# One-hot tiles a token at a time, gates stored expert by expert: the expert stage of a two-block network on one Trainium2 core

## The chip, the cores and the metric

The kernel runs on one core of a Trainium2 chip. The metric is the device time of one launch in microseconds, and lower is better. The core has a TensorE for matrix products, VectorE and ScalarE (ACT) and GpSimd (POOL) for the rest, and DMA queues that SyncE, ACT and POOL issue to. The times given are medians of several launches.

## What is computed

The reference is a pipeline of two blocks on 512 tokens of 1024 features, all in float32. The first has two layers of retention and attention with a feed-forward part. The second has a gated delta rule beside a recurrent unit, a cross attention into a memory, and a layer of retrieved experts, to which the change belongs:

```python
def peer_ffn(h, wq, subkeys, u_tab, v_tab):
    q = (t @ wq).reshape(ntok, 8, 2, 128)                    # 8 heads, two halves of a query
    sc = einsum('thpd,hpkd->thpk', q, subkeys)               # against 128 first and 128 second keys
    s1, i1 = top_k(sc[:, :, 0], 16); s2, i2 = top_k(sc[:, :, 1], 16)
    best, pos = top_k(s1[..., :, None] + s2[..., None, :], 16)     # of 256 pairs
    idx = e1 * 128 + e2                                      # e1, e2: i1, i2 at pos // 16, pos % 16
    gate = softmax(best)
    act = gelu(einsum('phkd,pd->phk', u_tab[idx], t)) * gate
    return einsum('phk,phkd->pd', act, v_tab[idx])
```

There are 16384 experts (128 first keys times 128 second keys), and a token uses 8 x 16 of them.

## The kernel before

**The expert stage.** The tokens stand in four blocks of 128. The last block gathers its experts' rows by indirect DMA. The first three (384 tokens, dense) are multiplied with both whole tables: `first_product(j)` is the product of the 128 experts of first key j with the dense tokens (24 passes 384 wide, as each float32 operand is carried as a high and a low part), and `second_product` adds up the second table's rows. Between them stands a factor for every expert and token: the token's gate where it uses the expert, zero elsewhere.

**The choices** (2384 to 2523 us). `choose` finds a head's 16 best pairs for 128 tokens on VectorE. At its end the keys of the chosen pairs are picked out of a list: a 16x16 comparison (L1692), a multiplication on POOL (L1694), and a reduction over 16 on VectorE (L1695). It runs for all eight heads of the first block and for four heads of the second and third. The others, eight in all, run during the spreading, and eight more for the gathered block later.

**The spreading** (2523 to 2765 us). `spread(n)` makes the table of factors of a dense block. A token's factors over 128 first and 128 second keys are a product of two matrices that the token's 128 choices index: `oa` has a row for each choice with its gate at the place of the second key, `ob` a one at the place of the first key. `ones_hot` makes both for four tokens at a time (32 blocks for each n, 96 in all): two comparisons on VectorE, 512 wide, of the row `io` (0 to 127) with the choice's key (L1774, L1775). The gate is then multiplied into `oa`, in every second block by four activations on ACT (L1778), in the others by one operation on POOL (L1780). Two blocks later TensorE multiplies the four tokens' `oa` and `ob` into a bank of PSUM (L1795), ACT moves it to a staging tile `st` (L1797), and after eight blocks SyncE stores that to DRAM as `gd` (L1801). Products of the first table fill TensorE in between. Their tile of weights is split by `load_w`: the high part by ACT (L243), the low part by POOL here, and by VectorE for the third block of tokens (L244).

**The second tables** (from 2765 us). `prepare(j)` loads `gin` from `gd` for four first keys at a time, multiplies the acts of tile j by it (L1873), and splits the result (L331 on ACT, L332 on VectorE). `second_product` (L1883) follows. The gathered block's rows come in beside it (L1853, L1859, L1862).

Each engine takes its instructions in the order in which they were given to it. A tile's buffers are written again only when their readers are done.

Of the kernel before, what the change touches and what calls it, by code (L numbers as in the profile page):

```python
# [29 lines left out]
# ------------------------------------------------------------------ host side: layout only  # L30
def _wtiles(w):
    """[K, M] -> [M/128, 128, (K/128)*128]; each tile holds all of K for 128 columns."""
    k, m = w.shape
    return w.reshape(k // 128, 128, m // 128, 128).transpose(2, 1, 0, 3).reshape(m // 128, 128, -1)


def _vtiles(w):
    """[1024, N] -> [(N/256)*2, 128, 4*256]; halves of K for 256 columns."""
    n = w.shape[1]
    return w.reshape(2, 4, 128, n // 256, 256).transpose(3, 0, 2, 1, 4).reshape(-1, 128, 1024)  # L40
# [24 lines left out]
def _vec(a):  # L65
    """[..., 128*n] -> [128, ..., n]"""
    a = a.reshape(a.shape[:-1] + (-1, 128))
    return np.moveaxis(a, -1, 0)
# [52 lines left out]
def _blockdiag(w):  # L121
    """[8, 64, 64] -> [128, 4, 128]: two blocks to a chunk"""
    o = np.zeros((4, 128, 128), w.dtype)
    o[:, :64, :64] = w[0::2]
    o[:, 64:, 64:] = w[1::2]
    return o.transpose(1, 0, 2)
# [29 lines left out]
# ------------------------------------------------------------------ the program  # L156
def interleave(*gens):
    """Emit the steps of several strands in turns; a pair gives a strand and its steps to a turn."""
    live = [g if isinstance(g, tuple) else (g, 1) for g in gens]
    while live:  # L160
        for g in list(live):
            if any(next(g[0], "end") == "end" for _ in range(g[1])):
                live.remove(g)
# [22 lines left out]
def _program(tc, I, out, dbg, upto, layers, pools):  # L186
# [32 lines left out]
    def rsqrt_small(dst, src, scale):  # L219
        """dst = (src*scale + EPS)^-0.5 for a narrow [p, n]."""  # L220
# [6 lines left out]
    def load_w(src=None, sub=None, pool=None, into=None):  # L227
        """a tile of weights, as the sum of two that a pass each carries"""
# [18 lines left out]
    def pieces(p, n):  # L247
        """[128, n] in a tile of PG, as pieces of up to a bank"""
        return [p[:, 0, :HN], p[:, 1, :HN]] if n == L else [p[:, 0, :n]]

    def PV(p, n):
        """the same, as one"""
# [23 lines left out]
    def fed_gemms(feed_c, u, n, fills=()):  # L276
        """Products of the next three tiles of weights with u, following its chunks as feed_c writes them, after
        other ones that wait for nothing; returns what they are in, as pieces of up to a bank."""
# [35 lines left out]
    # ---------------------------------------------------------------- first block  # L314
# [9 lines left out]
    def V2(t):  # L324
        """what matches PV"""
        return t.rearrange("p (a b) -> p a b", a=2) if t.shape[1] == L else t

    def split(dh, dl, src, g=None, on=None):
        """dh + dl = src (* g)"""
# [27 lines left out]
    def cols6(acc, scale):  # L357
        """rsqrt(mean over partitions) per token, blocks of tokens as columns"""
# [8 lines left out]
    def bcast6(r6):  # L367
        """the same as rows, all partitions alike: slices of the tokens and where they are"""
# [26 lines left out]
    def cols(acc, scale, n):  # L395
        """rsqrt(mean over partitions) per token, [128, n/128]"""
# [7 lines left out]
    def bcast(r):  # L404
        """[128, k] -> rows [128, k*128] in PSUM, the same on all partitions"""
# [20 lines left out]
    # the memory's keys and values, a tile at a time where the first block leaves the tensor engine room  # L426
# [32 lines left out]
    def memory_values(ng, mem):  # L459
        """two steps"""  # L460
# [19 lines left out]
    # the first layer's input, and its first products  # L480
# [7 lines left out]
    def products_aside(feed_c, n, scale=1.0, fills=(), room=None):  # L488
        """the first four tiles of a phase, put aside until the tokens' scales are there"""
# [27 lines left out]
    for l in range(layers):  # L517
# [3 lines left out]
        # from here on the last layer leaves the first tokens out, except as keys and values  # L521
# [5 lines left out]
        # ============================================================ phase A  # L527
# [10 lines left out]
        # distances: between tokens of a block, and down a column to the block's ends  # L538
# [11 lines left out]
        # decays of a block's keys towards its end and its start, and of a whole block (of the sums from the  # L550
        # tokens before in the upper half, from those after in the lower)
# [6 lines left out]
        # what turns the distances' decays into those to a block's ends  # L558
# [3 lines left out]
        # the tokens' scales as columns, for the blocks of TB  # L562
# [12 lines left out]
        # the attention's keys, split in two: the first parts of a group twice, the rests once  # L575
# [3 lines left out]
        # a block of queries makes room for its own outputs; the other half holds what retention cycles through  # L579
        QA = OA = QO[:, 0]  # L580
        spare = QO[:, 1].rearrange("p a b -> p (a b)")
        # keys of one head of a chunk, with zeros for the other; a head's queries with both decays
# [7 lines left out]
        def scaled(tab):  # L590
            """a table times the tokens' scales"""
# [34 lines left out]
        # values, turned to token-major; the retention's minus their mean over a head's features, so that  # L626
        # its outputs have mean zero
# [24 lines left out]
        # the first tokens' values of a group, block diagonal over its heads  # L652
# [16 lines left out]
        # ---- projections that fill in: queries and keys of the attention, then the retention's gates  # L669
# [25 lines left out]
        # ---- retention: within a block of tokens as it stands, between blocks by the decayed sums of keys  # L695
        # times values over the blocks before and after
        def retention():
# [35 lines left out]
            def turn(c):  # L733
                """a chunk's keys, token-major"""
# [67 lines left out]
        # ---- attention over the first tokens and a band  # L802
        def halves(qb):
            """a block's queries, a group's first parts and rests above each other"""
# [123 lines left out]
        # ============================================================ phase B  # L928
# [59 lines left out]
        def spaced_rs(ss, name, fills):  # L988
            """the tokens' scales, with other products between their steps"""
# [77 lines left out]
        if l == layers - 1:  # L1067
            # the delta rule's decays and steps
# [9 lines left out]
    # ---------------------------------------------------------------- second block  # L1078
# [28 lines left out]
    def softplus(dst, x, n):  # L1107
        """log(1 + exp(x)) = max(x, 0) + 2 atanh(e / (2 + e)), e = exp(-|x|)"""
# [15 lines left out]
    # decay and step of a token and head as columns, [128, 4 (block), 4 (head)]  # L1124
# [30 lines left out]
    def conv(dst, p, w, bias=None, on=None, soon=False):  # L1155
        """causal taps along the tokens of p * row scale"""
# [31 lines left out]
    def gate(c, p):  # L1188
        """the delta rule's"""
# [61 lines left out]
    # ---- the remaining projections fill in: the recurrence's input and gate, the delta rule's gate  # L1251
# [19 lines left out]
    # ---- the gated delta rule, a block of 128 tokens and four heads at a time; what a block needs of the  # L1271
    # others comes last, and replaces its queries, keys and values
    def inside(n, e):
# [31 lines left out]
        # the inverse of I + A, and its transpose, by doubling of the blocks  # L1305
# [101 lines left out]
    # ---- the gated linear recurrence  # L1407
# [47 lines left out]
    # ---- out of the mixer: the first tiles, over the recurrence's outputs, while the delta rule ends  # L1455
# [51 lines left out]
    # ---- attention into the memory  # L1507
# [84 lines left out]
    # ---- product-key experts: the first three blocks of tokens against the whole tables, the last by gathers  # L1592
    def head_queries(h):
        """of a head, both sides; without the tokens' scales"""
# [26 lines left out]
    gd = dr.tile([ND, 128, 32, 128, 4], F32, name="gd")  # L1621
# [30 lines left out]
    def sixteens(pool):  # L1652
        """0 to 15 down, the same along"""
# [5 lines left out]
    def selection(pool, bufs):  # L1659
        """the tiles of a block's choices: their sums, and the keys of both sides"""  # L1660
# [4 lines left out]
    def choose(pool, sel, h, sc):  # L1665
        """the 16 best pairs of keys of a head, of scores [128, 2, 128]"""
# [28 lines left out]
        nc.vector.tensor_reduce(keys[:, :, h], oh.rearrange("p s j k -> p s k j"), axis=AX.X, op=OP.add)  # L1695

    def soften(n, best):
        """softmax over a head's 16, of scores still without the tokens' scales, in place"""
# [8 lines left out]
    # acts of a tile of 128 experts (one first key) for the dense tokens  # L1707
# [22 lines left out]
    BYACT = lambda k: k % 2 == 0  # L1730
    sels = [selection(p1, ND) for n in range(ND)]
    fill = iter(range(LA))
    # the first block's choices come first; the second and third one's last four heads wait till it is spread
# [26 lines left out]
    # the experts' weights of a block's tokens, spread over all experts: [second key, first key, token]  # L1760
    def spread(n):
# [8 lines left out]
        def ones_hot(b, by_act):  # L1770
            oa = p1.tile([128, 4, 128], F32, name="oa", tag="oa", bufs=5)
            ob = p1.tile([128, 4, 128], F32, name="ob", tag="ob", bufs=5)
            iot = io[:, None, :].to_broadcast([128, 4, 128])
            nc.vector.tensor_tensor(oa, iot, sl[:, 2, b:b + 4, None].to_broadcast([128, 4, 128]), op=OP.is_equal)  # L1774
            nc.vector.tensor_tensor(ob, iot, sl[:, 1, b:b + 4, None].to_broadcast([128, 4, 128]), op=OP.is_equal)  # L1775
            if by_act:
                for t in range(4):
                    nc.scalar.activation(oa[:, t], oa[:, t], AF.Copy, scale=sl[:, 0, b + t:b + t + 1])  # L1778
            else:
                nc.gpsimd.tensor_tensor(oa, oa, sl[:, 0, b:b + 4, None].to_broadcast([128, 4, 128]), op=OP.mult)  # L1780
# [3 lines left out]
        for k in range(32 + LEAD):  # L1784
            if k < 32:
                hot.append(ones_hot(4 * k, BYACT(k)))
# [3 lines left out]
            if m % 8 == 0:  # L1790
                st = p1.tile([128, 32, 32, 4], F32, name="stg", tag="stage", bufs=2)
# [5 lines left out]
            nc.scalar.activation(st[:, :, t0:t0 + 4], pg4.rearrange("p (t g e) -> p g t e", t=4, e=4), AF.Copy)  # L1797
# [161 lines left out]
```

## Time and profile before

| | us |
|---|---|
| time, median of 3 runs | 3728.36 |
| lowest and highest of the 3 | 3717.03, 3739.03 |
| the profiled execution: its span, first to last instruction | 3726.1 |

The profiled execution's own launch time is not listed apart from the three; its span is 2.3 us below their median.

The page gives each engine's busy time over the span. A table of stretches gives it stage by stage, with the granted clock of TensorE and the share of the DMA engines. The waits say which engine waited for whose result. Groups of instructions say how often an operation ran and its mean time, in which waiting for a shared resource is included; start-to-start times in the timeline show what an instruction really takes of its engine, as the next one starts before the end of the one ahead is recorded.

### The profile page before, as it was taken

The page shows a single profiled execution, that of the slowest core. Times are in us where ns is not written, and L with a number is a line of the kernel's source. Part 1 is how long each engine was busy: PE and PEld are TensorE (multiplying, and loading weights), DVE is VectorE, ACT ScalarE, POOL GpSimd, SP SyncE. Part 2 cuts the span into 40 slices and gives each one's busy share as a digit, 9 for nine tenths or more (in the row PEclk, how much of TensorE's full clock was granted, in tenths as well). Part 3 has the DMA queues.
Part 4 walks back from the last instruction along what each step waited for, and adds up shares of the span by engine and source line. Part 5 has one row for each costly group of instructions (what it writes and reads, how often), then busy time and mean ns, then how long its engine had stood idle before and what let it go on. Part 6 is the DMA issues. An engine that isn't in the chain of part 4 may idle for free. (4 is left out here: it accounts for less than half of the span.)

```text
span 3726.1 us, 54318 instructions
## 1 busy us (share of the span) xinstructions
PE 3586.0 (96%) x21341; PEld 3212.1 (86%) x21341; DVE 2413.2 (65%) x4258; ACT 1494.8 (40%) x2675; POOL 946.7 (25%) x708
## 2 busy tenths in 40 slices
PE   8999999999999999999999999997889999999998
PEld 8989999999997888788878877887778999999987
DVE  7554436333656454633467755689979988888875
ACT  4454324222444432422344453425553434434333
POOL 4211112000422111200032330446433334333321
PEclk9988999999998999999999999998999999999999
DMA  4101232222320033322232131323468878888855
GB/s 138 58 23 41 93 119 97 90 89 89 124 86 29 30 105 116 101 96 96 93 123 68 35 96 55 116 86 119 130 209 323 338 304 320 315 320 324 317 212 181
DMA packets 185887, 531.42 MB, mean 143 GB/s; under 512 B 16416, under 2 KB 70048, under 8 KB 168992
## 3 DMA queue, kind: packets, MB, share of 16 engines
q1 hardware_dynamic: 150272, 367.67, 29.6%
q0 software_dynamic: 18432, 134.23, 9.1%
q10 hardware_dynamic: 16928, 26.06, 2.1%
q8 instruction: 168, 2.75, 0.3%
q14 instruction: 87, 0.71, 0.1%
HBM read 492.64 MB, written 35.19 MB: 142 GB/s over the span
## 5 line engine op out<-in xcount | busy, mean ns | idle before, releaser
L243 ACT ACTIVATE whi<-wraw 128x1024 fp32r<-128x1024 f32 x594 | 627.6, 1058 | 1043.0 <-PE g L263 628.3
L244 DVE TENSOR_TENSOR wlo<-wraw,whi 128x1024 fp32r<-128x1024 f32 x543 | 680.5, 1254 | 294.9 <-ACT whi L243 287.6
L263 PE MATMUL g<-uh,whi 128*128 128x264 f32 (+1 forms) x1864 | 476.1, 318 | 4.6 <-ACT z L605 4.6
L263 PE MATMUL g<-uh,wlo 128*128 128x264 f32 (+1 forms) x1864 | 468.7, 314 | 1.3 <-DVE wlo L244 1.3
L263 PE MATMUL g<-ul,whi 128*128 128x264 f32 (+1 forms) x1864 | 468.8, 314 | 0.0
L350 POOL TENSOR_TENSOR ssq<-ssq,sq 128x512 f32<-128x512 f32 (+2 forms) x84 | 133.4, 1588 | 926.1 <-issue 715.8
L1721 PE MATMUL f<-TH,wlo 128*128 128x384 f32 x1024 | 348.8, 341 | 5.4 <-POOL wlo L244 5.4
L1721 PE MATMUL f<-TH,whi 128*128 128x384 f32 x1024 | 350.8, 343 | 1.2 <-ACT stash L1722 1.1
L1721 PE MATMUL f<-TL,whi 128*128 128x384 f32 x1024 | 347.5, 339 | 0.0
L263 PEld LDWEIGHTS g<-uh,whi 128*128 128x128 f32 x1864 | 308.4, 192 | 25.4 <-ACT z L605 5.0
L263 PEld LDWEIGHTS g<-uh,wlo 128*128 128x128 f32 x1864 | 307.7, 191 | 21.4 <-DVE wlo L244 1.6
L263 PEld LDWEIGHTS g<-ul,whi 128*128 128x128 f32 x1864 | 308.2, 191 | 19.6 <-issue 1.3
L1904 POOL COPY pace<-al 1x1 f32<-1x1 f32 x128 | 109.4, 855 | 563.6 <-DVE al L332 561.8
L1883 PE MATMUL acc<-whi,ah 128*128 128x512 f32 x768 | 240.1, 394 | 7.3 <-ACT whi L243 6.4
L1883 PE MATMUL acc<-wlo,ah 128*128 128x512 f32 x768 | 238.9, 392 | 4.1 <-DVE wlo L244 4.1
L1883 PE MATMUL acc<-whi,al 128*128 128x512 f32 x768 | 238.5, 392 | 0.0
L263 PE MATMUL g<-Hh,wlo 128*128 128x264 f32 (+1 forms) x768 | 203.9, 320 | 0.0
L263 PE MATMUL g<-Hl,whi 128*128 128x264 f32 (+1 forms) x768 | 203.8, 320 | 0.0
L263 PE MATMUL g<-Hh,whi 128*128 128x264 f32 (+1 forms) x768 | 203.4, 319 | 0.0
L1853 POOL DMA_INDIRECT gtile<-in_uv_dram,ix x128 | 189.8, 1483 | 46.4 <-issue 27.4
L1721 PEld LDWEIGHTS f<-TH,whi 128*128 128x128 f32 x1024 | 196.2, 192 | 5.8 <-ACT stash L1722 1.9
L1721 PEld LDWEIGHTS f<-TH,wlo 128*128 128x128 f32 x1024 | 195.5, 191 | 6.4 <-POOL wlo L244 6.4
(588 smaller groups left out, 7608.3 us busy)
## 6 DMA issues: line engine op xcount, KB each, us to landing
wraw<-in_w_dram SPq DMA_DIRECT2D x340, 512.0 KB, 3.5
wraw<-in_uT_dram SPq DMA_DIRECT2D x128, 512.0 KB, 5.6
wraw<-in_uv_dram SPq DMA_DIRECT2D x128, 512.0 KB, 4.9
gd<-stg SPq DMA_DIRECT2D x12, 2048.0 KB, 9.9
gin<-gd SPq DMA_DIRECT2D x32, 768.0 KB, 11.2
h0c<-in_h_dram SPq DMA_DIRECT2D x8, 264.0 KB, 4.3
H<-in_h_dram ACTq DMA_DIRECT2D x8, 264.0 KB, 5.9
hs<-H ACTq DMA_DIRECT2D x8, 264.0 KB, 2.1
```

The source lines that it names most:

```text
L243: nc.scalar.activation(hi, raw, AF.Copy)
L244: (sub or nc.vector).tensor_tensor(lo, raw, hi.bitcast(F32), op=OP.subtract)
L263: nc.tensor.matmul(pw, wt[:, sl], xt[:, kc, hf * w_:(hf + 1) * w_], start=(first and n == 0 and a == 0), stop=(last and n == len(kcs) - 1 ...
L350: nc.gpsimd.tensor_tensor(self.acc, self.acc, t, op=OP.add)
L1721: nc.tensor.matmul(p[:, :NT], wt[:, sl], x[:, kc], start=(kc == 0 and a == 0), stop=(kc == 7 and a == 2))
L1853: nc.gpsimd.indirect_dma_start(out=gtile, out_offset=None, in_=I["uv"], in_offset=bass.IndirectOffsetOnAxis(ap=ix[:, k:k + 1], axis=0))
L1883: nc.tensor.matmul(accs[2 * n + q], x[:, tk], wt[:, 512 * q:512 * q + 512], start=(j == 0 and k == 0), stop=(j == 127 and k == 2))
L1904: after = nc.gpsimd.tensor_copy(pace, ready[2][0:1, 0:1].bitcast(F32)).ins
```

## The change

It touches four places, all in the expert stage. `ones_hot` makes the tiles for one token at a time: for each of four tokens one scalar operation 128 wide compares `io` with the key of each partition and multiplies by the gate, and one compares with the other key. The activations on ACT and the multiplications on POOL are gone. The staging tile, `gd` and `gin` put a first key's tokens next to each other, in runs of 32, where four first keys alternated token by token. The product with `gin` reads those runs. In `choose`, the reduction over 16 becomes four additions that halve the list each time. Comments and docstrings are removed as well, which lie outside the program that the chip runs.

```diff
-    gd = dr.tile([ND, 128, 32, 128, 4], F32, name="gd")
+    gd = dr.tile([ND, 128, 32, 4, 128], F32, name="gd")
...
-        nc.vector.tensor_reduce(keys[:, :, h], oh.rearrange("p s j k -> p s k j"), axis=AX.X, op=OP.add)
+        for n in (8, 4, 2):
+            nc.vector.tensor_tensor(oh[:, :, :n], oh[:, :, :n], oh[:, :, n:2 * n], op=OP.add)
+        nc.vector.tensor_tensor(keys[:, :, h], oh[:, :, 0], oh[:, :, 1], op=OP.add)
...
-    BYACT = lambda k: k % 2 == 0
...
-        def ones_hot(b, by_act):
+        def ones_hot(b):
             oa = p1.tile([128, 4, 128], F32, name="oa", tag="oa", bufs=5)
             ob = p1.tile([128, 4, 128], F32, name="ob", tag="ob", bufs=5)
-            iot = io[:, None, :].to_broadcast([128, 4, 128])
-            nc.vector.tensor_tensor(oa, iot, sl[:, 2, b:b + 4, None].to_broadcast([128, 4, 128]), op=OP.is_equal)
-            nc.vector.tensor_tensor(ob, iot, sl[:, 1, b:b + 4, None].to_broadcast([128, 4, 128]), op=OP.is_equal)
-            if by_act:
-                for t in range(4):
-                    nc.scalar.activation(oa[:, t], oa[:, t], AF.Copy, scale=sl[:, 0, b + t:b + t + 1])
-            else:
-                nc.gpsimd.tensor_tensor(oa, oa, sl[:, 0, b:b + 4, None].to_broadcast([128, 4, 128]), op=OP.mult)
+            for t in range(4):
+                k = slice(b + t, b + t + 1)
+                nc.vector.tensor_scalar(oa[:, t], io, sl[:, 2, k], sl[:, 0, k], op0=OP.is_equal, op1=OP.mult)
+                nc.vector.tensor_scalar(ob[:, t], io, sl[:, 1, k], None, op0=OP.is_equal)
             return oa, ob
...
-                hot.append(ones_hot(4 * k, BYACT(k)))
+                hot.append(ones_hot(4 * k))
...
-                st = p1.tile([128, 32, 32, 4], F32, name="stg", tag="stage", bufs=2)
+                st = p1.tile([128, 32, 4, 32], F32, name="stg", tag="stage", bufs=2)
...
-            nc.scalar.activation(st[:, :, t0:t0 + 4], pg4.rearrange("p (t g e) -> p g t e", t=4, e=4), AF.Copy)
+            nc.scalar.activation(st[:, :, :, t0:t0 + 4], pg4.rearrange("p (t g e) -> p g e t", t=4, e=4), AF.Copy)
...
-                nc.sync.dma_start(gd[n, :, :, 32 * q:32 * q + 32], st)
+                nc.sync.dma_start(gd[n, :, :, q], st.rearrange("p g e t -> p g (e t)"))
...
-            gins[0] = p2.tile([128, ND, 128, 4], F32, name="gin", tag="gin", bufs=2)
-            nc.sync.dma_start(gins[0], gd[:, :, j // 4].rearrange("n p t e -> p n t e"))
+            gins[0] = p2.tile([128, ND, 4, 4, 32], F32, name="gin", tag="gin", bufs=2)
+            nc.sync.dma_start(gins[0].rearrange("p n q e t -> p n (q e t)"),
+                              gd[:, :, j // 4].rearrange("n p q x -> p n (q x)"))
...
-        nc.vector.tensor_mul(a, a, gins[0][:, :, :, j % 4].rearrange("p n t -> p (n t)"))
+        a4 = a.rearrange("p (n q t) -> p n q t", n=ND, q=4)
+        nc.vector.tensor_mul(a4, a4, gins[0][:, :, :, j % 4])
```

## Rows read from the trace of the kernel before

**Rows 1.** The page's busy time, share of the span and instructions of each engine.

```profile
PE 3586.0 (96%) x21341; PEld 3212.1 (86%) x21341; DVE 2413.2 (65%) x4258; ACT 1494.8 (40%) x2675; POOL 946.7 (25%) x708
```

**Rows 2.** Stages: stretch, length, busy PE, PEld, DVE, ACT, POOL; clock, DMA share, GB/s.

```profile
2384.00:2523.00 139.00, 126.73 (x649) 111.71 (x648) 124.61 (x527) 44.88 (x69) 68.58 (x38) 0.97 0.29 95
2523.00:2700.00 177.00, 144.83 (x891) 139.19 (x890) 167.30 (x355) 98.42 (x228) 98.01 (x54) 0.90 0.42 125
2700.00:2765.00 65.00, 56.14 (x391) 54.57 (x389) 59.33 (x68) 45.36 (x111) 29.83 (x19) 0.95 0.60 179
2765.00:2900.00 135.00, 124.53 (x614) 112.00 (x613) 112.24 (x175) 47.39 (x77) 38.32 (x30) 0.96 0.90 317
2900.00:3713.00 813.00, 812.07 (x4021) 727.97 (x4020) 677.98 (x1103) 324.60 (x538) 278.52 (x236) 1.00 0.78 293
```

**Rows 3.** Waits, 2518 to 2768: who waited for whom, us in total, times, longest.

```profile
POOL oa L1780 <- DVE oa L1774: 59.7, 33, 3.7
...
PE s L1795 <- POOL oa L1780: 23.2, 17, 4.3
...
DVE oa L1774 <- PE s L1795: 4.7, 2, 3.1
```

**Rows 4.** Groups of instructions, 2518 to 2768: busy us, mean ns, idle before.

```profile
L1795 PE MATMUL s<-ob,oa 128*128 128x128 f32 x768 | 111.0, 299 | 37.8 <-POOL oa L1780 23.2 <-DVE ob L1775 8.4 <-ACT oa L1778 3.0
...
L1774 DVE TENSOR_TENSOR oa<-io,sl 128x512 f32<-128x512 f32 x96 | 100.1, 1043 | 5.0 <-PE s L1795 4.7 <-ACT sl L1768 0.3
L1775 DVE TENSOR_TENSOR ob<-io,sl 128x512 f32<-128x512 f32 x96 | 79.6, 829 | 0.0
L1780 POOL TENSOR_TENSOR oa<-oa,sl 128x512 f32<-128x512 f32 x48 | 74.7, 1557 | 82.3 <-DVE oa L1774 59.7 <-ACT oa L1778 10.9 <-PE s L1795 8.3
...
L244 POOL TENSOR_TENSOR wlo<-wraw,whi 128x1024 fp32r<-128x1024 f32 x18 | 44.9, 2496 | 20.8 <-ACT whi L243 20.8
```

**Rows 5.** Timeline of the last blocks: start us, us, engine, instruction.

```profile
2741.52 1.36 POOL L1780 TENSOR_TENSOR oa<-oa,sl 128x512 f32<-128x512 f32 x1 [1.29 <-DVE oa L1774]
2741.90 1.52 DVE L1774 TENSOR_TENSOR oa<-io,sl 128x512 f32<-128x512 f32 x1
2743.34 0.68 DVE L1775 TENSOR_TENSOR ob<-io,sl 128x512 f32<-128x512 f32 x1
...
2745.15 1.52 DVE L1774 TENSOR_TENSOR oa<-io,sl 128x512 f32<-128x512 f32 x1
```

**Rows 6.** Timeline of VectorE early in the kernel: two of the retention's decays.

```profile
33.30 0.27 DVE L715 TENSOR_SCALAR t<-dist,nex 128x128 f32<-128x128 f32 x1
33.50 0.27 DVE L717 TENSOR_SCALAR t<-dist,ex 128x128 f32<-128x128 f32 x1
```

**Rows 7.** Two lines of the convolutions: count, ns minimum/median/maximum, first and last start.

```profile
L1164 DVE TENSOR_SCALAR tw<-cv,convw x12: 472/476/1572, 1942.8 to 2025.1; 128x512 f32<-128x512 f32 x12
L1166 DVE TENSOR_SCALAR XG<-cv,lconvw,lvec x4: 529/546/1493, 2042.2 to 2082.7; 128x512 f32<-128x512 f32 x4
```

**Rows 8.** Timeline: POOL's split of a weight tile beside a scalar operation.

```profile
2670.83 2.41 POOL L244 TENSOR_TENSOR wlo<-wraw,whi 128x1024 fp32r<-128x1024 f32 x1 [2.95 <-ACT whi L243]
...
2671.50 1.77 DVE L1686 TENSOR_SCALAR ab<-ii 128x16 uint32<-128x16 uint32 x1
```

**Rows 9.** Timeline of VectorE in the choices: a head's reduction and what follows.

```profile
2506.20 1.07 DVE L1695 TENSOR_REDUCE keys<-oh 128x32 f32<-128x512 bf16 x1 [1.23 <-POOL oh L1694]
2507.19 0.28 DVE L1673 MAX8 vv<-s 128x8 f32<-128x128 f32 x1
```

**Rows 10.** Two lines of the second tables, columns as in Rows 7.

```profile
L1873 DVE TENSOR_TENSOR stash<-stash,gin x128: 821/842/871, 2782.5 to 3581.1; 128x384 f32<-128x384 f32 x128
...
L332 DVE TENSOR_TENSOR al<-stash,ah x128: 539/556/573, 2784.7 to 3710.8; 128x384 fp32r<-128x384 f32 x128
```

**Rows 11.** TensorE's waits from 2768 to the end, columns as in Rows 3.

```profile
PE acc L1883 <- ACT whi L243: 6.4, 1, 6.4
PE acc L1883 <- DVE wlo L244: 4.1, 4, 2.1
```

## The prediction

> **What bounds the kernel now.** I read the page's busy shares first. TensorE is busy for 96% of the span [rows 1], so over most of the kernel shorter work on another engine buys nothing, and only stretches in which TensorE waits can pay. The table of stages finds them [rows 2]. From 2900 to 3713 TensorE is busy for 812.07 of 813 us. Before that are four stretches with gaps: the choices (2384 to 2523, 12.3 us without TensorE), the spreading of the gates (2523 to 2765, 41.0 us), and the start of the second tables (2765 to 2900, 10.5 us). The change lies in these, above all in the spreading. There VectorE is busy for 167.30 + 59.33 = 226.6 of 242 us, while ACT and POOL have room. The waits say the same as a chain [rows 3]: TensorE's products of one-hot tiles wait 23.2 us for POOL's gated tile, and POOL waits 59.7 us for VectorE's comparison. VectorE itself waits only 4.7 us there for TensorE to free a tile. So VectorE sets the pace of the spreading.
>
> The groups of that stretch say what VectorE does [rows 4]: 96 pairs of 512-wide comparisons, oa and ob, mean 1043 and 829 ns. The timeline of the last blocks shows how such a pair is paid [rows 5]. Two blocks take 2745.15 - 2741.90 = 3.25 us. One oa lasts 1.52 us: it started while POOL multiplied the previous oa, and ended 0.54 us after POOL did. The other three take (2745.15 - 2743.34)/3 = 0.60 us from start to start, at 0.68 us each. So a pair costs 1.20 us of VectorE, and what POOL takes away comes on top: (1043 - 680) x 96 + (829 - 680) x 96 = 49 us over the stage. POOL is busy for 74.7 us with the gate and 44.9 us with the weights' low parts [rows 4]; the loss is 49/119.6 = 0.41 us for each of POOL's.
>
> **The one-hots.** For each block of four tokens two 512-wide comparisons become eight instructions 128 wide: four with one scalar per partition (ob), four with two (oa). The nearest rows are the retention's decays, 128 wide in float32, one per-partition scalar: 0.20 us from start to start, 0.27 each [rows 6]. The second scalar is priced by two lines 512 wide: 476 ns median with one, 546 with two [rows 7], so 0.06 us from the two minima and 0.07 from the medians. I take 0.20 for ob and 0.26 for oa: 4 x 0.46 = 1.84 us a block, against 1.20. Over 96 blocks that is 176.6 against 115.2: **+61 us** of VectorE. Bounds: 0.20 for both gives +38; 0.28 for oa, its scalar priced a little dearer than the medians say, gives +69.
>
> **What POOL and ACT give back.** The gate is multiplied in the same instruction, so POOL's 48 multiplications (74.7 us) and ACT's 192 activations go. ACT's time is worth nothing by itself, as it has room [rows 2]. POOL's matters through what it takes from VectorE. The low parts of the weights, 18 at about 2.5 us, stay on POOL [rows 4]. A scalar operation is held by them as well: one 16 wide, started 0.67 us into such a subtraction, lasted 1.77 us and ended when POOL did [rows 8]. At today's share POOL still takes 0.41 x 44.9 = 18 us: **-31 us**. If each subtraction held VectorE almost to its end, at a share of 0.9, 40 us stay and the gain is -9; if none did, it is -49. I take the first, since the choices' instructions lie between the one-hots in two of the three blocks of tokens as they do today.
>
> **The keys' sums.** A reduction costs VectorE 2507.19 - 2506.20 = 0.99 us a head [rows 9]. Four additions of 256, 128, 64 and 32 elements replace it. At 0.20 us each, as for the 128-wide ones [rows 6], they cost 0.8; I estimate 0.6, since the two last are short: -0.4. Each needs the one before, so with nothing to put between them they could cost as much as the reduction. Eight heads are chosen while the spreading runs: **-3 us** (0 to -5). In the stage of choices lie 16; VectorE is busy there for 124.61 of 139 us and TensorE waits only at the end, so what VectorE saves moves the start of the spreading: **-6 us** (0 to -10).
>
> **The spreading in sum.** +61 - 31 - 3 = +27 on VectorE; its 4.7 us of waiting for TensorE [rows 3] should go, as TensorE then has the more room: **+23 us**. TensorE's work is unchanged: 768 passes of the one-hot products [rows 4] and the first products between them, 144.83 + 56.14 = 201 us busy of 242.
>
> **The stage's output.** ACT's eviction stg keeps 512 elements but reads PSUM in steps of 128 and writes runs of four. No row shows such a reading. Between 0 and a doubling of its 96 evictions I take 0: even a doubling is about what the removed activations free, on an engine that is busy for 98.42 of 177 us [rows 2]. It would be late only if it took longer than VectorE takes for a block. The stores of gd still move runs of 512 bytes and the loads of gin 2048 bytes, twelve and 32 of them: no cost either way, by the indices. No wait is added on another queue.
>
> **The gathering stage.** The product of acts and gates reads gin in steps of four elements today and lasts 842 ns; the subtraction of the same 128x384 shape with dense operands lasts 556 [rows 10]. After the change gin is read in runs of 32, so I take 556: 128 x 0.29 = 37 us less of VectorE. Nearly all of it is hidden behind TensorE, which does not wait from 2900 on [rows 2]. What can be won are its waits ahead of that: 4.1 us for the weights' low parts, which queue behind these products on VectorE, and a bit of the 6.4 us at the start [rows 11], where two such products lie ahead of ACT's first whi: **-5 us** (-1 to -7). If runs of 32 were as slow as steps of four, it is 0.
>
> **Sum.** +23 - 6 - 5 = +12 us. The profiled execution spans 3726.1 us; the median of the three times is 3728.4, so 2.3 us lie around the span, which I keep. 3728.4 + 12 = **3740 us**.
>
> **Rivals.** *Slower: POOL's subtractions hold VectorE to their end.* Nearly all of VectorE's instructions then are scalar operations like the one in [rows 8]. At a share of 0.9, 22 us more are lost: 3762. It decides once the share passes some 0.57, that is, 7 us more. For it: that row, and the last block of tokens, where no choices lie between. Against it: today's comparisons are held as well, and the mean is 0.41.
>
> *About as before: scalar operations are held less.* If POOL no longer takes time from them, 18 us fall away: 3722, and 3714 with the best ends of the keys' sums and the gathering. Against it stands the same row.
>
> *Much faster: the small tiles cost only their share.* If 128 elements cost a quarter of a 512-wide comparison's 0.60, so 0.15, eight make 1.2 us a block, today's price, and only the gains remain: VectorE falls by 31 + 3 to 192 us, below TensorE's 201. TensorE becomes the bound, the spreading shortens by some 41 us, and with the other 11 the time is 3676. For it: at 512 wide a scalar operation is cheaper than the comparison, 476 ns against 680. Against it: [rows 6] shows 0.20 at just this shape.
>
> [...]
>
> *The change does not do what it says.* Whether the additions beat the reduction and whether runs of 32 are fast are the two places; with both at 0 the 3 + 6 + 5 us fall away and the time is 3754.
>
> **Chances.** About 0.5% (18.6 us) is what a measurement of this kernel can tell from no change. The forecast, with its own range of 3728 to 3752, 0.50 (0.36 same, 0.14 slower). Held to the end, 0.22, all slower. Held less, 0.12 (0.11 same, 0.01 faster). Cheap small tiles, 0.13, faster. The rest 0.03 (same 0.02, faster 0.01). So faster 0.15, same 0.49, slower 0.36. The range leaves out the cheap tiles below and a few parts in a hundred above: 3710 to 3768.
>
> **What would show it.** Right: one-hot instructions at about 0.28 and 0.34 us, 0.20 and 0.26 from start to start; VectorE full from 2523 on for some 265 us, with TensorE waiting for VectorE's oa and ob instead of POOL's oa; some 45 us of weights' low parts on POOL with stretched one-hots beside them; the product with gin near 556 ns; four additions well under 0.99 us. Wrong: if the small instructions follow each other at 0.15 us or less, if VectorE has gaps in the spreading, if ACT's eviction grows past a block's time, or if the low parts of the weights arrive so late behind VectorE's scalar operations that the first products wait.

## The result and the profile after

The changed kernel takes 3779.9 us (median of four runs, 3774.86 to 3781.76); the kernel before takes 3728.0 beside it. The ratio is 1.014, with an interval of 1.0117 to 1.0163: **slower by 52 us**. The forecast was 3740 us and a range of 3710 to 3768; the time lies above the range.

The first line of the page, columns as in [rows 1]:

```profile
PE 3617.5 (96%) x21341; PEld 3219.0 (85%) x21341; DVE 2436.5 (64%) x4930; ACT 1444.6 (38%) x2483; POOL 881.7 (23%) x660
```

POOL lost its 48 gate multiplications and ACT its 192 activations. VectorE has 672 instructions more, but only 23 us more work. TensorE has the same 21341 instructions and is busy 31.5 us longer. That is no work added: in the spreading its 768 one-hot products keep their length (311 ns on average for 299), but lie further apart, so that their records overlap less and cover 163.3 us for 111.0.

To find the 52 us I cut both spans at the same three events: the first sum of keys, the first one-hot tile, and the last product of one-hot tiles. The rows are then the choices, the spreading of the gates, and everything behind it. The kernel before (columns as in [rows 2]):

```profile
2390.30:2523.20 132.90, 120.63 (x617) 106.56 (x616) 119.11 (x500) 40.54 (x62) 67.50 (x37) 0.96 0.28 92
2523.20:2763.20 240.00, 198.97 (x1268) 191.76 (x1268) 226.42 (x421) 142.50 (x336) 126.58 (x73) 0.91 0.47 141
2763.20:3726.00 962.80, 942.13 (x4659) 844.53 (x4657) 797.69 (x1293) 377.16 (x628) 319.73 (x270) 0.99 0.79 294
```

The kernel after:

```profile
2393.40:2557.80 164.40, 126.17 (x618) 109.12 (x617) 151.51 (x552) 40.56 (x62) 67.37 (x37) 0.94 0.24 74
2557.80:2822.50 264.70, 225.43 (x1275) 196.36 (x1275) 259.02 (x1018) 92.29 (x145) 50.00 (x25) 0.93 0.44 130
2822.50:3780.00 957.50, 940.07 (x4650) 842.14 (x4649) 756.04 (x1317) 376.42 (x626) 330.22 (x269) 0.99 0.79 295
```

| stretch | forecast | measured |
|---|---|---|
| up to the first sum of keys | 0 | +3.1 |
| choices | -6 | **+31.5** |
| spreading | +23 | +24.7 |
| behind it | -5 | -5.4 |
| span | +12 | +53.9 |

The spreading and the rest came out as forecast. Nearly the whole miss is in the choices, 37.5 of 41.9 us, where the change does nothing but replace a reduction by four additions. VectorE's busy time there grew by 32.4 us, as much as the stretch. The groups of VectorE in the choices of the kernel after (columns as in [rows 4]):

```profile
L1697 DVE TENSOR_TENSOR oh<-oh 128x256 bf16<-128x256 bf16 x16 | 38.8, 2424 | 10.3 <-POOL oh L1695 10.3
L1697 DVE TENSOR_TENSOR oh<-oh 128x128 bf16<-128x128 bf16 x16 | 13.5, 845 | 0.2
...
L1698 DVE TENSOR_TENSOR keys<-oh 128x32 f32<-128x32 bf16 x16 | 2.8, 177 | 0.2
L1697 DVE TENSOR_TENSOR oh<-oh 128x64 bf16<-128x64 bf16 x16 | 2.8, 176 | 0.2
```

The four lines add up to 57.9 us. In the kernel before, 16 reductions took 18.2 in the same stretch:

```profile
L1695 DVE TENSOR_REDUCE keys<-oh 128x32 f32<-128x512 bf16 x16 | 18.2, 1140 | 11.4 <-POOL oh L1694 11.4
```

The first addition, of 256 elements, takes 2.42 us on average, the last, of 32, 0.18. A timeline of one head in that stretch (start, length, engine, instruction, and in brackets the idle time before) says why:

```profile
2404.69 1.05 POOL L1695 TENSOR_TENSOR oh<-oh,fl 128x512 bf16<-128x512 bf16 x1 [6.55 <-DVE oh L1693]
...
2405.70 2.35 POOL L244 TENSOR_TENSOR wlo<-wraw,whi 128x1024 fp32r<-128x1024 f32 x1
2405.77 2.42 DVE L1697 TENSOR_TENSOR oh<-oh 128x256 bf16<-128x256 bf16 x1 [0.43 <-POOL oh L1695]
...
2408.39 0.21 DVE L1697 TENSOR_TENSOR oh<-oh 128x128 bf16<-128x128 bf16 x1
...
2408.73 0.17 DVE L1697 TENSOR_TENSOR oh<-oh 128x64 bf16<-128x64 bf16 x1
...
2409.12 0.17 DVE L1698 TENSOR_TENSOR keys<-oh 128x32 f32<-128x32 bf16 x1
```

The addition waits for POOL's multiplication `oh`. Behind that multiplication POOL's queue holds a subtraction of a weight tile's low part, which waits for nothing more. So both are released at once; POOL starts 0.07 us ahead, and the addition ends with the subtraction (2408.19 and 2408.05). Where a second subtraction follows, the second addition can be held too: in five of the 16 heads it lasts 2.1 to 2.3 us, in the others 0.20 to 0.22, and the 845 ns are the mean. The theory from here on: **POOL's subtractions hold the additions**, and one of them lies behind each of the 16 multiplications of this stretch.

The spreading, the groups of the kernel after:

```profile
L1793 PE MATMUL s<-ob,oa 128*128 128x128 f32 x768 | 163.3, 311 | 36.6 <-DVE ob L1778 35.0
...
L1777 DVE TENSOR_SCALAR oa<-io,sl 128x128 f32<-128x128 f32 x384 | 149.6, 390 | 2.9 <-ACT sl L1770 2.9
...
L1778 DVE TENSOR_SCALAR ob<-io,sl 128x128 f32<-128x128 f32 x384 | 122.9, 320 | 0.0
...
L244 POOL TENSOR_TENSOR wlo<-wraw,whi 128x1024 fp32r<-128x1024 f32 x17 | 40.5, 2385 | 143.8 <-ACT whi L243 71.1 <-PE s L1793 59.7 <-PE f L1724 8.7
```

and its waits, columns as in [rows 3]:

```profile
PEld s L1793 <- DVE ob L1778: 36.7, 82, 2.2
PE s L1793 <- DVE ob L1778: 35.0, 27, 2.8
```

TensorE now waits for VectorE's one-hot tiles directly, instead of POOL's gated ones [rows 3]. VectorE is busy for 259.02 of the stage's 264.70 us and still sets its pace.

### The profile page after: what moved, and what is told of

It reads as the page before. It is cut to its first block, busy times and chain, and to the rows that moved or that the text cites. A ratio compares the mean times of both kernels' runs of the same rounds, so it can differ in the third digit from the quotient of the medians.

```text
span 3780.0 us, 54665 instructions
## 1 busy us (share of the span) xinstructions
PE 3617.5 (96%) x21341; PEld 3219.0 (85%) x21341; DVE 2436.5 (64%) x4930; ACT 1444.6 (38%) x2483; POOL 881.7 (23%) x660
## 5 line engine op out<-in xcount | busy, mean ns | idle before, releaser
L1724 PE MATMUL f<-TH,wlo 128*128 128x384 f32 x1024 | 356.5, 348 | 11.6 <-POOL wlo L244 9.9
L1904 POOL COPY pace<-al 1x1 f32<-1x1 f32 x128 | 130.5, 1020 | 556.8 <-DVE al L332 480.0
L1857 DVE SCALAR_TENSOR_TENSOR gtile<-gtile,TT 128x1024 f32<-128x1024 f32 x128 | 155.8, 1217 | 73.1 <-DMA gtile<-in_uv_dram,ix 73.1
```

The lines of the kernel that those rows point to most:

```text
L1724: nc.tensor.matmul(p[:, :NT], wt[:, sl], x[:, kc], start=(kc == 0 and a == 0), stop=(kc == 7 and a == 2))
L1857: nc.vector.scalar_tensor_tensor(gtile[:, :D], gtile[:, :D], 1.0, TT, op0=OP.mult, op1=OP.mult, accum_out=ac)
L1904: after = nc.gpsimd.tensor_copy(pace, ready[2][0:1, 0:1].bitcast(F32)).ins
```

## Experiments

The first four kernels were timed beside the kernel before at 3732.5 us, the last four at 3739.4. The kernel before thus took 4 and 11 us more there than the 3728 from which the expected times were worked out, so a measured time says less than its ratio. The parts of the change come first, each undone or done alone. The stretches of each kernel's profiled execution, cut at the same events, in us:

| kernel | choices | spreading | behind it | median | ratio to before |
|---|---|---|---|---|---|
| before | 132.9 | 240.0 | 962.8 | 3732.5 / 3739.4 | |
| after (beside 3728.0) | 164.4 | 264.7 | 957.5 | 3779.9 | 1.0140 |
| reduction back | 132.9 | 267.8 | 950.6 | 3740.8 | 1.0032 |
| additions alone | 164.3 | 246.3 | 975.9 | 3774.5 | 1.0108 |
| runs alone | 133.1 | 244.4 | 957.0 | 3728.7 | 0.9989 |
| one-hots alone | 134.3 | 267.4 | 964.5 | 3755.7 | 1.0053 |
| low parts on VectorE in the choices | 139.4 | 266.5 | 953.3 | 3751.0 | 1.0032 |
| low parts on VectorE in the spreading | 132.8 | 251.0 | 956.0 | 3727.5 | 0.9974 |
| a quarter fused | 132.8 | 207.4 | 957.3 | 3686.4 | 0.9860 |
| first addition on POOL | 141.4 | 210.4 | 959.3 | 3694.9 | 0.9888 |

The stretch ahead of the choices, which is not in the table, varies between 2380.9 and 2397.8 us from profile to profile, with no pattern that follows the edits. So a stretch is compared with the same stretch, and whole times by their medians.

**The reduction put back.** All the rest of the change stays.

```diff
-for n in (8, 4, 2):
-    nc.vector.tensor_tensor(oh[:, :, :n], oh[:, :, :n], oh[:, :, n:2 * n], op=OP.add)
-nc.vector.tensor_tensor(keys[:, :, h], oh[:, :, 0], oh[:, :, 1], op=OP.add)
+nc.vector.tensor_reduce(keys[:, :, h], oh.rearrange("p s j k -> p s k j"), axis=AX.X, op=OP.add)
```

> The changed kernel with the reduction of choose in place of the four additions, all else as changed. Theory (the additions are held by POOL's subtractions of the weights' low parts, 16 times some 2.4 us ahead of the spreading): the spreading starts near 2523 us again instead of 2558 and lasts some 265 us, time 3738 to 3745. Rival (the spreading starts late for another reason, such as the smaller work between the one-hots or the new layout): the start stays near 2558, time 3775 or more.

Measured: 3740.8 us, ratio 1.0032 (1.0019 to 1.0046). The choices fall back to 132.9 us, the spreading keeps its 267.8. The additions alone thus made the choices longer. The timeline of this kernel shows the reduction in the very place in which the addition was held:

```profile
2391.25 1.05 POOL L1695 TENSOR_TENSOR oh<-oh,fl 128x512 bf16<-128x512 bf16 x1 [3.89 <-DVE oh L1693]
2392.26 2.41 POOL L244 TENSOR_TENSOR wlo<-wraw,whi 128x1024 fp32r<-128x1024 f32 x1
...
2392.34 1.16 DVE L1696 TENSOR_REDUCE keys<-oh 128x32 f32<-128x512 bf16 x1 [0.43 <-POOL oh L1695]
```

It starts 0.08 us behind the subtraction and lasts 1.16 us all the same; the longest of the 16 lasts 1.166. POOL does not hold this reduction.

**The additions alone**, in the kernel before; the diff is the one above, reversed.

> The kernel before with the four additions alone. Theory: the spreading starts 30 to 35 us later, the first addition lasts 2.4 us on the mean instead of the 0.28 us of its size, time 3758 to 3768. Rival (the additions are harmless by themselves): start at 2523, time 3725 to 3730.

Measured: 3774.5 us, ratio 1.0108 (1.0086 to 1.0129), so 42.0 us from the additions, more than was expected. The 8.3 of the run without them and these 42.0 make 50.3, of the 52 that the change costs. The choices take 164.3 us, 31.4 more than before, and the first additions a mean of 2425 ns there:

```profile
L1696 DVE TENSOR_TENSOR oh<-oh 128x256 bf16<-128x256 bf16 x16 | 38.8, 2425 | 10.3 <-POOL oh L1694 10.3
```

In the spreading the eight first additions take 1197 ns on average, for 292 of the eight behind it, so some are held there as well, and it takes 6.3 us more. The stretch behind the spreading is 13 us longer than before in this profile, which neither theory explains.

**The runs alone**: `gd`, `stg` and `gin` in the new order, with the one-hot tiles and the reduction of before.

```diff
-st = p1.tile([128, 32, 32, 4], F32, name="stg", tag="stage", bufs=2)
+st = p1.tile([128, 32, 4, 32], F32, name="stg", tag="stage", bufs=2)
...
-nc.vector.tensor_mul(a, a, gins[0][:, :, :, j % 4].rearrange("p n t -> p (n t)"))
+nc.vector.tensor_mul(a4, a4, gins[0][:, :, :, j % 4])
```

> The kernel before with the new layout of the gates alone (staging tile, gd, gin). Theory: the product with gin falls from 842 to 551 ns, and from the end of the spreading to the end of the kernel it takes some 5 us less, time 3721 to 3725. Rival (all of it hidden behind TensorE): 3728.

Measured: 3728.7 us, ratio 0.9989 (0.9974 to 1.0003). The stretch behind the spreading is 5.8 us shorter in the profile, but the time's 3.8 us cannot be told from zero.

**The one-hots alone**, in the kernel before.

```diff
-nc.vector.tensor_tensor(oa, iot, sl[:, 2, b:b + 4, None].to_broadcast([128, 4, 128]), op=OP.is_equal)
-nc.vector.tensor_tensor(ob, iot, sl[:, 1, b:b + 4, None].to_broadcast([128, 4, 128]), op=OP.is_equal)
...
+for t in range(4):
+    k = slice(b + t, b + t + 1)
+    nc.vector.tensor_scalar(oa[:, t], io, sl[:, 2, k], sl[:, 0, k], op0=OP.is_equal, op1=OP.mult)
+    nc.vector.tensor_scalar(ob[:, t], io, sl[:, 1, k], None, op0=OP.is_equal)
```

> The kernel before with the one-hots per token alone. Theory: VectorE pays 1.81 us for a block of four tokens instead of 1.20 and is held by POOL's remaining subtractions, so the spreading lasts 263 to 269 us instead of 241 and starts where it did, time 3750 to 3757. Rival (the one-hots are harmless, the late start is all of the loss): 3728 to 3732.

Measured: 3755.7 us, ratio 1.0053 (1.0032 to 1.0074); its runs spread from 3742.2 to 3765.9, and the profiled one is the longest. The spreading takes 267.4 us, 27.4 more than before.

**The low parts on VectorE in the choices.** If POOL's subtractions hold the additions, taking them off POOL must free the additions, though VectorE then does the subtractions as well. The rival was that such additions are slow in themselves.

```diff
-            gemm2(p, load_w(sub=nc.gpsimd), uh, ul)
+            gemm2(p, load_w(), uh, ul)
...
-            first_product(next(fill), nc.gpsimd)
+            first_product(next(fill))
```

> The changed kernel, but while the choices run the low parts of the weights are subtracted on VectorE instead of POOL (head_queries and the first products of that loop). Theory (POOL's subtractions hold the additions): the first two additions fall from 2.42 and 0.85 us on the mean to about 0.28 and 0.21, which gives VectorE 44 us back; some twenty subtractions of 1.15 us cost it 23. From the first addition to the first one-hot 140 to 148 us instead of 164, time 3752 to 3768. Rival (four dependent additions are slow in themselves): they stay above 1 us and the time goes up by the 23 us, to 3795 or more.

Measured: 3751.0 us, ratio 1.0032 (1.0018 to 1.0046). The groups of VectorE in its choices:

```profile
L244 DVE TENSOR_TENSOR wlo<-wraw,whi 128x1024 fp32r<-128x1024 f32 x21 | 25.5, 1213 | 0.0
...
L1697 DVE TENSOR_TENSOR oh<-oh 128x256 bf16<-128x256 bf16 x16 | 6.8, 428 | 10.1 <-POOL oh L1695 10.1
...
L1697 DVE TENSOR_TENSOR oh<-oh 128x128 bf16<-128x128 bf16 x16 | 3.4, 214 | 0.1
```

The same 16 additions fall from 2424 to 428 ns, and 15 of them to 293: the sixteenth lasts 2.45, beside a subtraction of the spreading that stays on POOL ((16 x 428 - 2451)/15 = 293). VectorE took over 25.5 us of subtractions, and the choices still fell from 164.4 to 139.4 us, a little more than expected. The rival falls.

**The low parts on VectorE in the spreading**, with the reduction back in place: the same question for the one-hots.

```diff
-    OFF, AH, SUB, WH = 1, 1, nc.gpsimd, 4
+    OFF, AH, SUB, WH = 1, 1, nc.vector, 4
...
-        first_product(j, sub=nc.gpsimd)
+        first_product(j)
```

> The changed kernel with the reduction back, and the low parts of the weights of the spreading on VectorE instead of POOL. Theory (the 38 us by which the one-hots are stretched are POOL's subtractions): no one-hot lasts over 0.6 us apart from one behind POOL's multiplication of the choices, VectorE gives 38 us back and pays some 20, so the spreading lasts 246 to 253 us instead of 268, time 3717 to 3728. Rival (the small instructions are stretched by something else): the spreading becomes longer by 20, time 3755 or more.

Measured: 3727.5 us, ratio 0.9974 (0.9958 to 0.9991). The groups of VectorE in its spreading:

```profile
L1775 DVE TENSOR_SCALAR oa<-io,sl 128x128 f32<-128x128 f32 x384 | 134.2, 350 | 2.7 <-ACT sl L1768 2.7
L1776 DVE TENSOR_SCALAR ob<-io,sl 128x128 f32<-128x128 f32 x384 | 111.4, 290 | 0.0
L244 DVE TENSOR_TENSOR wlo<-wraw,whi 128x1024 fp32r<-128x1024 f32 x20 | 24.4, 1220 | 0.0
```

The means fall from 390 and 320 to 350 and 290 ns, and no one-hot lasts longer than 1.17 us, where some took 2.5. VectorE does 16 subtractions more, and the stage is 16.8 us shorter than with the reduction back alone. Still it stays 11 us longer than before. This run does not compare the small tiles with the large ones, as VectorE here does 20 us of subtractions that POOL did before (16 x 1.22); the next one does.

**A quarter fused.** A version built from these readings: the runs and the reduction, no low part on POOL in the spreading, `ob` always 512 wide, `oa` 512 wide with ACT's gates in three blocks of four, and only in the fourth the four fused instructions. POOL, which multiplied the gate in every second block before, multiplies none.

```diff
-    BYACT = lambda k: k % 2 == 0
+    BYACT = lambda k: k % 4 != 3
...
-                nc.gpsimd.tensor_tensor(oa, oa, sl[:, 0, b:b + 4, None].to_broadcast([128, 4, 128]), op=OP.mult)
+                for t in range(4):
+                    k = slice(b + t, b + t + 1)
+                    nc.vector.tensor_scalar(oa[:, t], io, sl[:, 2, k], sl[:, 0, k], op0=OP.is_equal, op1=OP.mult)
```

> A version built from the parts: the kernel before with the new layout; in three blocks of four the gate is multiplied by ACT, in the fourth oa comes from the fused instructions per token, ob always from the 512-wide comparison; POOL has neither the gate nor the low parts of the spreading. VectorE pays 1.20 us for three blocks and 1.64 for one, 126 us in all against 165 with its stretches today, and 20 us for the low parts. It falls to some 200 us, where TensorE's work of 185 to 201 us bounds the spreading: 200 to 215 us, time 3690 to 3705. Rival (ACT becomes the bound, with 36 times 1.3 us more): 235 us or more, 3720.

Measured: **3686.4 us, ratio 0.986 (0.9821 to 0.9898)**, faster than both kernels and than expected. The spreading takes 207.4 us, of which TensorE is busy for 190.08:

```profile
2521.60:2729.00 207.40, 190.08 (x1259) 181.51 (x1258) 194.73 (x512) 167.85 (x431) 14.55 (x8) 0.96 0.54 161
```

and its groups show the two prices side by side, both without POOL in the way:

```profile
L1783 DVE TENSOR_TENSOR ob<-io,sl 128x512 f32<-128x512 f32 x96 | 65.7, 685 | 0.0
...
L1776 DVE TENSOR_TENSOR oa<-io,sl 128x512 f32<-128x512 f32 x72 | 49.3, 684 | 1.0 <-ACT sl L1769 1.0
...
L1782 DVE TENSOR_SCALAR oa<-io,sl 128x128 f32<-128x128 f32 x96 | 28.5, 340 | 1.5 <-PE s L1798 1.5
```

The large comparisons, 1043 and 829 ns on average before [rows 4], take 684 and 685. Four fused instructions are 1.36 us of records a block, a large comparison 0.68. The run changes several things at once: how much of the gain is the quarter fused, how much the low parts and the gates that left POOL, and whether a version with no fused tile would do as well, no run separates.

**The first addition on POOL**, on top of that: if additions on VectorE are held, POOL could do the first, and VectorE reduce half as much. The rival was that waiting for POOL eats the gain.

```diff
+nc.gpsimd.tensor_tensor(oh[:, :, :8], oh[:, :, :8], oh[:, :, 8:], op=OP.add)
-nc.vector.tensor_reduce(keys[:, :, h], oh.rearrange("p s j k -> p s k j"), axis=AX.X, op=OP.add)
+nc.vector.tensor_reduce(keys[:, :, h], oh[:, :, :8].rearrange("p s j k -> p s k j"), axis=AX.X, op=OP.add)
```

> The version before this one, and in the choices the first of the halvings is done by POOL behind its multiplication; VectorE reduces 8 instead of 16. The reduction reads one input and was not held by POOL in any run so far. It should fall from 1.15 to some 0.6 us. From the first to the first one-hot 124 to 129 us instead of 133, time 5 to 9 us under the version before it. Rival (the longer way over POOL costs as much as the shorter reduction gains, as VectorE waits for POOL there): no change.

Measured: 3694.9 us, ratio 0.9888 (0.9857 to 0.9918), no better than without it. The reduction of half the elements falls from 1.14 to 0.64 us, but the waits of VectorE in the choices, of this kernel:

```profile
DVE keys L1697 <- POOL oh L1696: 19.3, 16, 4.1
```

were 11.5 us in the kernel without it. In the longest, a subtraction got between POOL's multiplication and its addition. So far the rival held: 7.9 us gained, 7.8 lost. But the choices also became 8.6 us longer, 141.4 for 132.8, and the expectation was 124 to 129. That goes with a hold of another instruction, 11.0 us more in all: `cd`, the float32 sum ahead of a head's pairs, takes 1289 ns on average for 600. That it now runs beside POOL's later subtraction is an inference from these means. Without and with the addition on POOL:

```profile
L1683 DVE TENSOR_TENSOR cd<-vv 128x256 f32<-128x256 f32 x16 | 9.6, 600 | 0.0
...
L1683 DVE TENSOR_TENSOR cd<-vv 128x256 f32<-128x256 f32 x16 | 20.6, 1289 | 0.0
```

## Why the prediction missed

**The step that failed: the keys' sums.** The prediction took four additions for 0.6 us a head, by the 128-wide decays [rows 6], and bounded their effect in the choices by 0 and -10 us. They cost +31.5. The price itself was nearer where nothing is in the way: in the spreading of the kernel after, the four take 281, 214, 180 and 180 ns, 0.85 us as records where the reduction took 1.10, so 0.25 us a head are saved for the 0.4 forecast. What was left out is that they are held. The prediction knew the hold, measured it as 49 us on the comparisons, and made its slower rival of it, but only for the one-hots. For the reduction it took the row's own 0.99 us [rows 9] as what an addition in its place would meet.

A row of before would have shown the difference. In the choices of the kernel before, beside the same POOL, no search shows a stretched time (0.26 to 0.31 us at 128 elements, 0.40 to 0.43 at 256) and no reduction (the 16 lie between 1.073 and 1.171 us), while `cd`, a float32 sum as the additions are sums, does. It stands so before, and below that in the kernel after:

```profile
L1682 DVE TENSOR_TENSOR cd<-vv 128x256 f32<-128x256 f32 x16 | 10.1, 632 | 0.0
...
L1683 DVE TENSOR_TENSOR cd<-vv 128x256 f32<-128x256 f32 x16 | 6.5, 408 | 0.0
```

Its mean is 632 ns where it was held, up to 1.40, and 408 where it was not. How long an addition would be held, the same trace says: each of the 16 reductions there starts 0.07 or 0.08 us behind the start of one of POOL's subtractions. With both, the bound for the additions would have been a hold by one subtraction a head, 16 x (2.42 - 0.28) = 34 us by the lengths measured since. That is on the side that the prediction excluded, and the range would have reached the measured time.

The bookkeeping of the choices: additions 57.9 for reductions 18.2, +39.7; `cd` held no longer, -3.6; together +36, of which VectorE's busy time, where records that overlap count once, shows 32.4. The stretch grew by 31.5, since nothing else in it had slack: TensorE waits there for POOL's low parts (23.4 us, 5.9 before), which queue behind multiplications that wait for VectorE, and at the end 8.9 us for the choices' result (4.8 before).

What a subtraction does beside the two is measured in the same place: 2.42 us on average for the addition that starts 0.07 or 0.08 us behind it, 1.14 on average for the reductions of before, which start 0.07 or 0.08 behind one too. Why the one is held and the other is not, no run shows. For the one-hots the order of the recorded starts did not decide it: in the spreading 7 of 17 subtractions began 0.01 to 0.10 us behind the one-hot that then lasted 2.4 us or more.

**Right by errors that cancel: the spreading**, +24.7 for +23. The one-hots' price was right: in a stretch without POOL four pairs start 1.81 us apart, forecast 1.84, and over 96 blocks that is +59 for +61. What POOL gives back was mis-sized: beside the medians of 335 and 275 ns, the 768 instructions lose 149.6 + 122.9 - 384 x 0.610 = 38 us to POOL's 50.0, a share of 0.77. The prediction's 0.41 leaves the choices' multiplications out of POOL's time; counted so, it is 38 of the low parts' 40.5, a share of 0.94. So -11 came back, not -31: for the one-hots the rival "held to the end", with 0.9 and -9, was right. Alone that would have cost 20 us more than forecast. Two gains that the forecast did not have offset it. Other VectorE instructions of the stage are held less than before (`cd` 6.5 to 2.8 us, `ab` 3.7 to 1.1, `fl` 5.0 to 2.5, `oh` 4.1 to 3.3: -9.6 together), and VectorE's idle time fell by 7.9 us (13.6 to 5.7), not 4.7. Eight heads' sums, 8.8 us as reductions, take 6.7 as additions, -2 for -3, and are not held there. The terms add up to +28; the 4 us to the measured 24.7 are not accounted for. That POOL's subtractions stretch the one-hots is shown by the run with the low parts on VectorE: POOL's time falls to 11 us, and the stage by 16.8.

**Right.** The product with `gin`: 551 ns for the forecast 556 [rows 10]. The line of the kernel after, columns as in [rows 7]:

```profile
L1873 DVE TENSOR_TENSOR stash<-stash,gin x128: 536/551/560, 2839.2 to 3635.2; 128x384 f32<-128x384 f32 x128
```

The stretch behind the spreading is 5.4 us shorter, forecast 5. TensorE's 6.4 us for ACT's first `whi` [rows 11] are gone; its wait for VectorE's `wlo` is 7.0 us, 4.1 before. As the runs alone gave a time that cannot be told from no change, these 5 us rest on profiles only, though on all of them: the stretch takes 950.6 to 959.3 us in the seven kernels with the new order and 962.8 to 975.9 in the three without. ACT's eviction with the new order takes a median of 597 ns, 586 before: no cost, as forecast.

**The other rivals.** "Held less" fell, as 38 us were lost to POOL where the share of before would have left 18. "Cheap small tiles" fell at 0.20 and 0.25 us from start to start. "The change does not do what it says" had the right place, the additions, but took no gain for its worst case, where the loss was 42 us.

**Left open.** The 13 us behind the spreading with the additions alone, what each part of the quarter-fused version gives, and how much of the low parts' gain over before (0.9974) comes from the runs.

## What to carry to other kernels

Before a reduction is replaced by shorter additions, look at what the other engine's queue holds behind the instruction that they wait for: here the same addition of 256 elements took 2.42 us in the choices and 0.28 in the spreading. A row of a similar instruction in the same stretch, its mean against its shortest, would have said so: `cd` took 632 ns on average and 404 at the least in the choices of before. And where a fused instruction takes work off other engines, compare its price at its width first: here four of them, 128 wide, took 1.36 us of records a block and the comparison 512 wide 0.68. Fusing all tiles made the spreading 27.4 us longer (ratio 1.0053), and the version that gained (0.986) fused a quarter of them and moved the low parts.

## What the runs showed of the hardware

- In the choices of the kernel after, in all 16 heads, POOL's subtraction behind its multiplication started 0.07 or 0.08 us before the first addition, which waited for that multiplication. Each of these additions was held, 2.41 to 2.46 us.
- The reduction of 512 elements was held in no run: 1.06 to 1.22 us, 32 times in each of the six kernels that have it. A one-hot with scalars from a tile was held like an addition: 2.45 us where it started 0.01 us ahead of a subtraction, for a median of 0.275, as two lines of the kernel after show:

```profile
2572.00 2.45 DVE L1778 TENSOR_SCALAR ob<-io,sl 128x128 f32<-128x128 f32 x1
2572.01 2.35 POOL L244 TENSOR_TENSOR wlo<-wraw,whi 128x1024 fp32r<-128x1024 f32 x1 [7.71 <-ACT whi L243]
```

- A second scalar per partition, with its multiplication, cost 0.05 us at 128 wide in the kernel after: from `ob` to `oa` 0.20 us, from `oa` to `ob` 0.25:

```profile
2689.74 0.28 DVE L1778 TENSOR_SCALAR ob<-io,sl 128x128 f32<-128x128 f32 x1
2689.94 0.34 DVE L1777 TENSOR_SCALAR oa<-io,sl 128x128 f32<-128x128 f32 x1
2690.19 0.28 DVE L1778 TENSOR_SCALAR ob<-io,sl 128x128 f32<-128x128 f32 x1
```
